# Block 1 of the output weights in tiles of another kind, in a one-core decoder layer

## The chip, the cores and the metric

One Trainium2 chip, one core. The time of a kernel is the device time of one launch in microseconds (us); the table gives the median of three runs. The profile is of one more execution, with its own time.

## The reference

One layer of a decoder on 1024 rows (and 16 learned rows ahead of them) of width 1024, all in float32:

```
u   = rmsnorm(h);  q, k, v, xr, yr = split(u @ w_in)
att = sliding-window attention with sinks (8 heads, 2 kv heads, window 128)
xr  = causal conv of width 4;  r, i = sigmoid(block-diagonal gates of xr)
hr  = scan h[t] = a[t] h[t-1] + sqrt(1 - a^2) * (i * xr),  a = exp(-8 r softplus(-lam))
h  += rmsnorm(concat(att, gelu(yr) * hr) @ w_out)
h  += rmsnorm(relu(rmsnorm(h) @ w_ff1)^2 @ w_ff2)
```

w_out is 1024 x 1024: eight blocks of 128 rows (kc = 0 to 7), of which 0 to 3 meet attention outputs and 4 to 7 meet the gated recurrence.

## The kernel before

Every float32 product is made of three products of a shorter format (`mm3`, lines 122 to 128): an operand is split into a high half, a cast on ScalarE (ACT, line 95) or VectorE (DVE, line 97), and a low half, the rest, always on DVE (line 98). Line 124 multiplies high by high, 125 and 126 the two mixed terms. So each block of w_out is loaded into a raw tile (`load_wo`, line 744, issued on SP's queue), its high half is cast, its low half is subtracted (`split_wo`), and then PE (TensorE) may use it in the output projection (`out_mm`, lines 787 to 797).

SBUF is cut into tiles of seven kinds, each with a fixed count (line 55): raw 2, ws 4, a 16, b 17, c 8, d 4, e 2. A tile is taken when a new name is given one of its kind, and it is free after the last reader of its old name. The 16 tiles a hold the normalized, transposed input u (high and low, 8 pairs) until the last projection of u is done. Of the two tiles e, one holds the raw gate weights (`graw`, line 683), until they are split, and the other their high half (`gh`, line 691), which PE reads in all four `gates(c)`.

The order on each engine isn't the order of the code: a scheduler orders the instructions of each engine when the program is built, from the priorities (the order of the code), the dependences and the release of tiles. Each engine then runs its own list strictly in order and waits for semaphores; a wait of one instruction holds all behind it on that engine. The projection of t = 0 to 3 uses two banks each of the four kinds of PSUM tiles (pt, o, acc, s) at once, since their first four blocks are given ahead (`out_mm(t, pos[t], range(4))`).

The time around the change: gates (PE, with sigmoids on ACT that empty the banks, line 82), the last projection y3 of u on PE with its copies on DVE (line 640), decay and recurrence (`decay`, `recur`: exponentials, square roots and table loads on ACT, products and scans on DVE, lines 728 to 730), gelu and gate products (line 736), then the output projection with a norm per 128 rows (`out_norm`, lines 803 to 825: squares at 810, scaling by the post-mix gain `gmix_b` at 816, adding x at 819, storing at 820, the second norm at 822 and 824) and transposes (`u2_tiles`: PE at 836, evictions on ACT at 847 and on DVE at 841). While it runs, the first FFN weights are loaded and split ahead (`early`, line 925).

Of the kernel before, what the change touches and what calls it, by code (L numbers as in the profile page):

```python
# [10 lines left out]
F32R = mybir.dt.float32r  # L11
# [5 lines left out]
P = 128  # L17
D = 1024
# [19 lines left out]
def hybrid_layer(  # L38
# [19 lines left out]
    def slot(tag, shape, dt=F32):  # L58
        uid[0] += 1
        return slab.tile(shape, dt, tag=tag, name=f"{tag}{uid[0]}", bufs=bufs[tag])  # L60

    def pair(tag, shape):
        return slot(tag, shape, F32R), slot(tag, shape, F32R)
# [29 lines left out]
    def split(hi, lo, src, eng=None):  # L93
        if eng is None:
            nc.scalar.copy(hi, src)  # L95
        else:
            eng.tensor_copy(hi, src)
        low = nc.vector.tensor_tensor(lo, src, f32(hi), op=ALU.subtract).ins  # L98
        mark[0] = low.name
        return low  # L100
# [648 lines left out]
    def split_wo(kc, tag, eng=None):  # L749
        wo[kc] = pair(tag, [P, D])  # L750
        split(wo[kc][0], wo[kc][1], wo_raw[kc], eng)
# [11 lines left out]
    load_wo(2, "d")  # L763
    load_wo(3, "raw")
    split_wo(0, "ws", nc.vector)
    for kc in range(1, 4):
        split_wo(kc, "a")
    for cp in (2, 3):
        at[0][cp] = pair("b", [P, 2, 512])
# [8 lines left out]
        rec_out(c, 1)  # L778


    gmix_b = slot("e", [P, D])
    nc.scalar.dma_start(gmix_b, g_post_mix[0].partition_broadcast(P))
    t4_dram = dpool.tile([P, 2, 4, 512], F32, name="t4_dram")

# [2 lines left out]
    def out_mm(t, po, kcs):  # L787
        half, o = t // 4, (t % 4) * P
        s = slice(o, o + P)
        for n in range(2):  # L790
            c = slice(512 * n, 512 * n + 512)
            for kc in kcs:
                ah, al = at[half][kc // 2]
                mm3(
                    po[n], (ah[:, kc % 2, s], al[:, kc % 2, s]),
                    (wo[kc][0][:, c], wo[kc][1][:, c]), kc == 0, kc == KC - 1,
                )

    def out_banks(t):
        tag = ("pt", "o", "acc", "s", "pt", "acc", "s", "pt")[t]  # L800
        return [bank(tag), bank(tag)]

    def out_norm(t, po):
        xr = slot("d", [P, D])
        nc.sync.dma_start(xr, x[t * P : (t + 1) * P, :])
        h = slot("raw", [P, D])
        ssq = [small.tile([P, 1], F32, name=f"sq{n}", tag=f"sq{n}") for n in range(2)]
        for n in range(2):
            c = slice(512 * n, 512 * n + 512)
            nc.scalar.activation(  # L810
                h[:, c], po[n], AF.Square, scale=RMS_SC, accum_out=ssq[n]
            )
        rs = rstd_of(ssq)
        for n in range(2):
            c = slice(512 * n, 512 * n + 512)
            nc.vector.scalar_tensor_tensor(
                h[:, c], po[n], rs, gmix_b[:, c], op0=ALU.mult, op1=ALU.mult
            )
        nc.vector.tensor_tensor(h, h, xr, op=ALU.add)
        nc.sync.dma_start(out[t * P : (t + 1) * P, :], h)  # L820
        ssq2 = small.tile([P, 1], F32, name="ssq", tag="ssq")
        nc.scalar.activation(xr, h, AF.Square, scale=RMS_SC, accum_out=ssq2)
        rs2 = rstd_of([ssq2])
        nc.vector.tensor_scalar(xr, h, rs2, None, op0=ALU.mult)
        return xr

    def u2_tiles(t, xn):
        half = t // 4
        if u2f[half][0] is None:
            u2f[half] = [slot("c", [P, 2, 512]) for _ in range(4)]  # L830
        o = (t % 4) * P
        for k4 in range(0, KC, 4):
            pt = bank("o", (P, 4, P))
            for i in range(4):
                kc = k4 + i
                nc.tensor.transpose(pt[:, i, :], xn[:, kc * P : (kc + 1) * P], ident)  # L836
            for i in range(0, 4, 2):
                kc = k4 + i
                dst = u2f[half][kc // 2]
                if k4:  # L840
                    nc.vector.tensor_tensor(
                        dst[:, :, o : o + P], pt[:, i : i + 2, :],
                        g_ffn_col[:, kc : kc + 2].to_broadcast([P, 2, P]), op=ALU.mult,
                    )
                    continue
                for n in range(2):
                    nc.scalar.activation(
                        dst[:, n, o : o + P], pt[:, i + n, :], AF.Copy,
                        scale=g_ffn_col[:, kc + n : kc + n + 1],
                    )  # L850
# [13 lines left out]
    def operand(tiles):  # L864
        pairs = []
        for t_ in tiles:
            hi, lo = pair("b", [P, 2, 512])
            split(hi, lo, t_)
            pairs.append((hi, lo))
        return pairs  # L870
# [54 lines left out]
    def early(b, p0, hl):  # L925
        raw = slot("raw", [P, 2, 4, P])
        for k in range(2):
            w1_load(raw[:, k], b, p0 + k, 0, 1)
        split(*hl, raw)
        return {p0 + k: (hl[0][:, k], hl[1][:, k]) for k in range(2)}  # L930
# [47 lines left out]
    ESH = [P, 2, 4, P]  # L978
# [11 lines left out]
    for t in range(8):  # L990
        po = pos[t] if t < 4 else out_banks(t)
        out_mm(t, po, range(4 if t < 4 else 0, KC))
        for t_ in {4: (0,), 5: (2,), 6: (4,), 7: (5,)}.get(t, ()):
            u2_tiles(t_, xns[t_])
        xns[t] = out_norm(t, po)
        for t_ in {4: (1,), 5: (3,), 7: (6,)}.get(t, ()):
            u2_tiles(t_, xns[t_])
        if t == 4:
            a11_early.update(early(0, 0, pair("a", ESH)))
        if t == 5:  # L1000
            b11 = operand(u2f[0][0:2])
            a12_early.update(early(1, 0, pair("ws", ESH)))
        if t == 6:
            b21 = operand(u2f[0][2:4])
            hl = slot("b", ESH, F32R), slot("e", ESH, F32R)
            a11_early.update(early(0, 2, hl))

    for p in range(2):
# [353 lines left out]
```

## Time and profile before

| what | value |
|---|---|
| time, median of 3 runs | 961.89 us (961.67 to 962.27) |
| time of the profiled execution | 959.9 us |
| span, first to last instruction | 957.9 us |
| granted TensorE clock, mean | 0.999 |
| busy: PE / DVE / ACT / POOL | 940.8 / 669.9 / 501.1 / 157.0 us |

The span is a little shorter than the time of the execution that it belongs to; what lies around it is launch and end. In the rows by time, a row has its start, its length, engine, line, operation, written and read tiles (buffer numbers left out), sizes, and in brackets the idle time of the engine before it with what ended it. A PE row is longer than the step from one matmul to the next, since matmuls overlap. The steps of such rows, not their lengths, tell PE's rate.

### The profile page before, as it was taken

The numbers are of one execution on the slowest core, as the hardware profiler recorded it, in microseconds if no ns is written. First come the engines' busy times: TensorE is split into PE (matmuls) and PEld (weight loads), VectorE is DVE, ScalarE is ACT, GpSimd is POOL, SyncE is SP. The second block draws the span as 40 slices with busy tenths as digits, with TensorE's granted clock in tenths as the row PEclk, the third lists the DMA queues.
The fourth block names the chain that finished last, engine by engine and source line by source line (L and its number), as shares of the span: only waits on it lengthen the run. The fifth ranks groups of instructions, "written<-read, shape, count | busy, mean of one in ns | idle before, by whom it ended". The sixth has DMA issues, their size and how long they took to land.

```text
span 957.9 us, 12381 instructions
## 1 busy us (share of the span) xinstructions
PE 940.8 (98%) x4654; PEld 789.2 (82%) x4654; DVE 669.9 (70%) x945; ACT 501.1 (52%) x822; POOL 157.0 (16%) x202
## 2 busy tenths in 40 slices
PE   7999999999999999999999999999999999999997
PEld 6999998888788877888888888888888888888886
DVE  5579989755955796575655556568557676779884
ACT  7556676469634563443555565654433343435441
POOL 4015656600021100000111001100111100003020
PEclk9999999999999999999999999999999999999999
DMA  8111101112235457675646466744677866567422
GB/s 289 51 49 41 38 9 45 38 62 67 87 133 176 141 181 236 190 260 188 212 154 219 155 195 188 234 156 122 161 181 191 199 219 195 178 193 159 112 87 88
DMA packets 85626, 140.74 MB, mean 147 GB/s; under 512 B 5784, under 2 KB 48936, under 8 KB 85568
## 3 DMA queue, kind: packets, MB, share of 16 engines
q1 hardware_dynamic: 75104, 108.51, 35.7%
q0 software_dynamic: 9600, 29.36, 11.9%
q10 hardware_dynamic: 864, 2.10, 0.6%
q8 instruction: 36, 0.59, 0.3%
q14 instruction: 22, 0.18, 0.1%
HBM read 115.70 MB, written 23.07 MB: 145 GB/s over the span
## 4 chain that ended last, share of the span: by engine, by line
PE 93%; ACT 3%; DVE 1%; issue 1%; DMA 0%; POOL 0%; DVEq 0%; SPq 0%; ACTq 0%
PE ps_acc L124 11%; PE ps_acc L125 11%; PE ps_acc L126 11%; PE ps_s L126 6%; PE ps_pt L124 6%; PE ps_s L125 6%; PE ps_s L124 6%; PE ps_pt L126 6%; PE ps_pt L125 6%; PE ps_o L124 5%; PE ps_o L126 5%; PE ps_o L125 5%; PE ps_o L585 1%; ACT c L82 1%; PE ps_o L836 1%
## 5 line engine op out<-in xcount | busy, mean ns | idle before, releaser
L95 ACT CAST ws<-raw 128x1024 fp32r<-128x1024 f32 (+1 forms) x70 | 71.8, 1026 | 120.5 <-PE ps_o L125 45.9
L98 DVE TENSOR_TENSOR ws<-raw,ws 128x1024 fp32r<-128x1024 f32 (+1 forms) x71 | 86.3, 1215 | 41.4 <-ACT ws L95 41.4
L124 PE MATMUL ps_acc<-a,ws 128*128 128x256 f32 (+2 forms) x256 | 85.2, 333 | 0.0
L125 PE MATMUL ps_acc<-a,ws 128*128 128x256 f32 (+2 forms) x256 | 84.9, 332 | 0.0
L126 PE MATMUL ps_acc<-a,ws 128*128 128x256 f32 (+2 forms) x256 | 84.8, 332 | 0.0
L98 DVE TENSOR_TENSOR b<-b,b 128x1024 fp32r<-128x1024 f32 (+2 forms) x48 | 57.6, 1201 | 29.3 <-PE ps_o L125 19.8
L95 ACT CAST ws<-e 128x1024 fp32r<-128x1024 f32 x42 | 43.9, 1045 | 58.2 <-PE ps_o L125 30.6
L95 ACT CAST b<-b 128x1024 fp32r<-128x1024 f32 (+2 forms) x48 | 49.4, 1030 | 35.0 <-DVE b L862 34.1
L98 DVE TENSOR_TENSOR ws<-e,ws 128x1024 fp32r<-128x1024 f32 x42 | 51.4, 1223 | 20.0 <-ACT ws L95 20.0
L575 POOL TENSOR_SCALAR_AFFINE_SELECT c<-c 128x512 fp32r<-128x512 f32 x64 | 55.7, 894 | 27.3 <-ACT c L95 15.3
L169 POOL TENSOR_TENSOR rs<-ms,half_pow 128x1 f32<-128x1 f32 (+1 forms) x29 | 21.3, 740 | 210.5 <-DVE ms L165 209.1
L126 PEld LDWEIGHTS ps_acc<-a,ws 128*128 128x128 f32 x256 | 48.2, 188 | 4.9
L124 PEld LDWEIGHTS ps_acc<-a,ws 128*128 128x128 f32 x256 | 48.2, 188 | 4.2
L125 PEld LDWEIGHTS ps_acc<-a,ws 128*128 128x128 f32 x256 | 48.2, 188 | 4.2
L124 PE MATMUL ps_acc<-ws,b 128*128 128x512 f32 (+1 forms) x120 | 46.3, 386 | 0.0
L125 PE MATMUL ps_acc<-ws,b 128*128 128x512 f32 (+1 forms) x120 | 46.1, 384 | 0.0
L126 PE MATMUL ps_acc<-ws,b 128*128 128x512 f32 (+1 forms) x120 | 46.0, 384 | 0.0
L125 PE MATMUL ps_pt<-ws,b 128*128 128x512 f32 x112 | 44.2, 395 | 0.6 <-DVE ws L98 0.6
L126 PE MATMUL ps_pt<-ws,b 128*128 128x512 f32 x112 | 43.9, 392 | 0.0
L124 PE MATMUL ps_pt<-ws,b 128*128 128x512 f32 x112 | 43.9, 394 | 0.0
L124 PE MATMUL ps_s<-ws,b 128*128 128x512 f32 x110 | 43.3, 395 | 0.0
L126 PE MATMUL ps_s<-ws,b 128*128 128x512 f32 x110 | 43.2, 393 | 0.0
(393 smaller groups left out, 2713.1 us busy)
## 6 DMA issues: line engine op xcount, KB each, us to landing
raw<-in_w_ff_dram SPq DMA_DIRECT2D x58, 512.0 KB, 4.3
e<-in_w_ff_dram SPq DMA_DIRECT2D x42, 512.0 KB, 4.1
raw<-in_w_in_dram SPq DMA_DIRECT2D x12, 512.0 KB, 3.9
d<-in_w_ff_dram SPq DMA_DIRECT2D x12, 512.0 KB, 3.8
s_dram<-d POOLq DMA_DIRECT2D x12, 512.0 KB, 3.9
e<-in_w_ff_dram POOLq DMA_DIRECT2D x10, 512.0 KB, 5.6
raw<-in_w_ff_dram POOLq DMA_DIRECT2D x10, 512.0 KB, 5.8
c<-in_x_dram SPq DMA_DIRECT2D x8, 512.0 KB, 8.1
```

The costliest lines, as they stand in the source:

```text
L82: ins = nc.scalar.activation(*args, **kwargs).ins
L95: nc.scalar.copy(hi, src)
L98: low = nc.vector.tensor_tensor(lo, src, f32(hi), op=ALU.subtract).ins
L124: nc.tensor.matmul(dst, lh, rh, start=start, stop=False, skip_group_check=True)
L125: nc.tensor.matmul(dst, lh, rl, start=False, stop=False, skip_group_check=True)
L126: last_mm[0] = nc.tensor.matmul(dst, ll, rh, start=False, stop=stop, skip_group_check=True).ins.name
L169: last_pow[0] = nc.gpsimd.tensor_tensor(rs[:n], ms[:n], half_pow[:n], op=ALU.pow).ins.name
L575: nc.gpsimd.affine_select(out=m[:, :, side, :], in_=f32(m)[:, :, 1, :], pattern=[[0, 4], [-sign, P]], compare_op=op, fill=0.0, base=0, cha ...
L585: nc.tensor.matmul(po[:, :, oc : oc + n], v, m[:, :, pc : pc + n], start=first and k == 0, stop=last and k == 1, skip_group_check=True,)
L836: nc.tensor.transpose(pt[:, i, :], xn[:, kc * P : (kc + 1) * P], ident)
```

## The change

Block 1 of w_out is split into the two tiles e instead of two tiles a: its high half takes the tile of the raw gate weights, its low half that of the high gate weights. Two later tiles go the other way: `gmix_b`, the post-mix gain spread over all partitions, and the low half of one early FFN block (`hl`) now take tiles a.

```diff
     split_wo(0, "ws", nc.vector)
-    for kc in range(1, 4):
+    split_wo(1, "e")
+    for kc in range(2, 4):
         split_wo(kc, "a")
...
-    gmix_b = slot("e", [P, D])
+    gmix_b = slot("a", [P, D])
     nc.scalar.dma_start(gmix_b, g_post_mix[0].partition_broadcast(P))
...
-            hl = slot("b", ESH, F32R), slot("e", ESH, F32R)
+            hl = slot("b", ESH, F32R), slot("a", ESH, F32R)
             a11_early.update(early(0, 2, hl))
```

Lines from 767 on carry a number higher by one after the change. No instruction is added or removed; the scheduler orders them otherwise. The first place is on ACT, from the gates to the end of the recurrence. raw_2758 is block 1, d_2760 block 2, raw_2762 block 3, d_2800 block 4:

```order
 L82 ACTIVATE c_2547<-ps_o_2558,prm 128x344
+L95 COPY e_2768<-raw_2758 128x1024
 L82 ACTIVATE c_2568<-ps_s_2569,prm 128x348
...
-L95 COPY a_2768<-raw_2758 128x1024
+L95 COPY a_2772<-d_2760 128x1024
 L82 ACTIVATE c_2605<-c_2605,m4sp 128x1040
 L82 ACTIVATE b_2745<-c_2642,m8sp 128x1040
-L95 COPY a_2772<-d_2760 128x1024
+L95 COPY a_2776<-raw_2762 128x1024
...
-L95 COPY a_2776<-raw_2762 128x1024
+L95 COPY a_2802<-d_2800 128x1024
```

Block 1's cast moves ahead among the sigmoids of the gates, and each of the blocks 2, 3 and 4 moves into the place of the one before it. On DVE the low halves move in the same way (2769 before the last gate product of line 715, then 2773, 2777 and 2803 each one place up). The cast of block 4 is followed by those of 5 to 7, behind which now stands the DMA of gmix_b (line 783 after the change), which stood before the gates.

The second place is PE at the start of the output projection, before the change (ps_pt_2849 and ps_pt_2850 are the two banks of the first 128 rows, ws_2764 and ws_2765 block 0, a_2768 and a_2769 block 1, b_946 and b_947 the first attention outputs):

```order
L125 MATMUL ps_pt_2849<-ws_2765,b_946 128x512
L126 MATMUL ps_pt_2849<-ws_2764,b_947 128x512
L124 MATMUL ps_pt_2849<-a_2768,b_946 128x512
L125 MATMUL ps_pt_2850<-ws_2765,b_946 128x512
L126 MATMUL ps_pt_2850<-ws_2764,b_947 128x512
L124 MATMUL ps_pt_2850<-a_2768,b_946 128x512
L125 MATMUL ps_o_2851<-ws_2765,b_946 128x512
```

and after it:

```order
L125 MATMUL ps_pt_2849<-ws_2765,b_946 128x512
L126 MATMUL ps_pt_2849<-ws_2764,b_947 128x512
L124 MATMUL ps_pt_2849<-e_2768,b_946 128x512
L125 MATMUL ps_pt_2849<-e_2769,b_946 128x512
L126 MATMUL ps_pt_2849<-e_2768,b_947 128x512
L124 MATMUL ps_pt_2849<-a_2772,b_1683 128x512
L125 MATMUL ps_pt_2850<-ws_2765,b_946 128x512
```

A bank now goes through blocks 0 and 1 and into block 2 before PE takes the next bank; before, PE went through six banks with block 0 and returned for block 1.

The third place is ACT during the norms, after the change (raw_3247 and raw_3366 are early FFN weights, ps_o_3191, 3229 and 3302 the first halves of the first three transposes):

```order
L848 ACTIVATE c_3188<-ps_o_3191,gcol 128x128 x2
L95 COPY a_3245<-raw_3247 128x1024
L823 ACTIVATE d_3207,ssq<-raw_3209 128x1024
L848 ACTIVATE c_3187<-ps_o_3229,gcol 128x128 x2
L848 ACTIVATE c_3188<-ps_o_3229,gcol 128x128 x2
L811 ACTIVATE raw_3320,sq_3321<-ps_acc_3252 128x512
L811 ACTIVATE raw_3320,sq_3322<-ps_acc_3253 128x512
L95 COPY ws_3364<-raw_3366 128x1024
L848 ACTIVATE c_3187<-ps_o_3302,gcol 128x128 x2
```

Before the change, the cast into a_3245 stood behind the eviction of ps_o_3229 and behind the square into d_3207, and the cast into ws_3364 behind the eviction of ps_o_3302. On SP the store of the fourth 128 rows (raw_3117) now stands ahead of the load of the fifth rows of x (d_3207), where it stood behind it.

## The prediction

> **What bounds the kernel now.** I read the head of the page first, then the waits of PE, then windows of single stages, and last the time-ordered rows of ACT, DVE and PE around the output projection. The page's first lines:
>
> ```profile
> span 957.9 us, 12381 instructions
> PE 940.8 (98%) x4654; PEld 789.2 (82%) x4654; DVE 669.9 (70%) x945; ACT 501.1 (52%) x822; POOL 157.0 (16%) x202
> ```
>
> PE is busy for all but 17.1 us. The change adds and removes no matmul, so it can win only gaps of PE, or add new ones. The view of the waits names the gaps (us in total, times, longest):
>
> ```profile
> PE ps_s L286 <- DVE d L213: 5.8, 1, 5.8
> PE ps_s L525 <- DVE negm L545: 1.7, 2, 1.3
> ...
> PE ps_acc L124 <- ACT a L1059: 0.7, 1, 0.7
> PE ps_pt L124 <- ACT a L95: 0.6, 1, 0.6
> PE ps_pt L125 <- DVE ws L98: 0.6, 1, 0.6
> ```
>
> The first two lie before the output projection, out of the change's reach. The last two are it: PE waits once for the high half of an output-weight block (ACT, L95) and once for a low half (DVE, L98). Windows of the stages (PE, PEld, DVE, ACT, POOL busy, then clock and DMA):
>
> ```profile
> 230.00:245.00 15.00, 13.96 (x60) 10.70 (x58) 15.00 (x14) 14.94 (x19) 0.00 (x0) 1.00 0.35 107
> 245.00:350.00 105.00, 104.89 (x487) 86.09 (x488) 76.94 (x110) 55.20 (x118) 12.91 (x25) 1.00 0.46 152
> 360.00:940.00 580.00, 580.00 (x2540) 472.42 (x2539) 387.74 (x404) 275.16 (x321) 52.83 (x61) 1.00 0.61 181
> ```
>
> Between 230 and 245 us ACT (14.94 of 15) and DVE (15.00 of 15) are both full and PE is not; that is the stage where one cast more or less decides. Afterwards PE is full again to the end, so microseconds gained by 245 should arrive at the end one for one, if no new gap opens.
>
> **The change, part by part.** The two gaps on PE:
>
> ```profile
> 231.98 0.63 PE L124 MATMUL ps_s<-ws,b 128*128 128x512 f32 x2
> 233.16 0.50 PE L125 MATMUL ps_pt<-ws,b 128*128 128x512 f32 x1 [0.56 <-DVE ws L98]
> 245.11 0.73 PE L124 MATMUL ps_pt<-a,b 128*128 128x512 f32 x2 [0.58 <-ACT a L95]
> ```
>
> *The high halves on ACT.* In the new order block 1 is cast between two sigmoids of the gates, and blocks 2, 3 and 4 take the places that blocks 1, 2 and 3 had.
>
> ```profile
> 203.96 0.58 ACT L82 ACTIVATE c<-ps_o,prm 128x344 f32<-128x344 f32 x1
> 206.12 0.55 ACT L82 ACTIVATE c<-ps_s,prm 128x348 f32<-128x348 f32 x1 [1.58 <-PE ps_s L126]
> 230.55 1.03 ACT L95 CAST a<-raw 128x1024 fp32r<-128x1024 f32 x1
> 233.60 1.04 ACT L95 CAST a<-d 128x1024 fp32r<-128x1024 f32 x1
> 244.03 1.03 ACT L95 CAST a<-raw 128x1024 fp32r<-128x1024 f32 x1
> ```
>
> The three last rows are blocks 1, 2 and 3. ACT idles from 204.54 to 206.12, 1.58 us, and the moved cast takes 1.03: hidden, if its data are there. Its load is the second of two rows merged here, with the time to landing of the eight loads of output weights under it:
>
> ```profile
> 189.78 10.43 SPq L744 DMA_DIRECT2D raw<-in_w_out_dram  x2
> DMA to landing us min/median/max: 3.2/3.2/4.1
> ```
>
> The second issue ends at 200.21, so it lands by about 204.3, just in time. Should it be 1 or 2 us late, the sigmoids behind it wait, and PE asks for their banks again only at the next set:
>
> ```profile
> 210.35 0.32 PE L124 MATMUL ps_s<-b,e 128*128 128x348 f32 x1
> ```
>
> That is 3.7 us after the bank's eviction ends at 206.67, so I cost this move at nothing; without that cover it is at most the cast's 1.03. Block 3's cast now stands at 233.60 instead of 244.03. Its load waits for block 1's raw tile, which is free after the early low half (below, 219.4); landing by 223.6, it is early by 10 us. PE's gap at 244.53 therefore goes: **0.58 us gained**. What stands at 244.03 now is block 4. Its load waits for block 2's tile, whose low half moves from 238.13 to 233.02 on DVE (next rows), so it is issued near 234.3 and lands by 238.4, ahead of 244.03.
>
> *The low halves on DVE.*
>
> ```profile
> 218.91 1.24 DVE L715 TENSOR_TENSOR c<-c,b 128x1040 f32<-128x1040 f32 x1 [3.69 <-ACT c L82]
> 221.79 0.69 DVE L640 COPY d<-ps_acc 128x512 f32<-128x512 f32 x1 [1.63 <-PE ps_acc L126]
> 231.89 1.22 DVE L98 TENSOR_TENSOR ws<-raw,ws 128x1024 fp32r<-128x1024 f32 x1
> 233.02 1.22 DVE L98 TENSOR_TENSOR a<-raw,a 128x1024 fp32r<-128x1024 f32 x1
> 238.13 1.22 DVE L98 TENSOR_TENSOR a<-d,a 128x1024 fp32r<-128x1024 f32 x1
> ```
>
> Block 1's low half needs the other tile of kind e, which holds the gate weights until the last gate product, about 218.1. It runs from there to 219.4 and pushes the L715 behind it by about 0.5 us, to 220.6; DVE then idles until 221.79 anyway. Cost: nothing. Block 0's low half (231.89, tile ws) keeps its place behind the same recurrence steps, so PE's other gap, 0.56 us, **stays**.
>
> *PE.* From the L125 at 233.16 on, both orders have 89 matmuls before the first one of block 4; the new order only uses blocks 0 to 3 bank by bank. The rows of before and the next block's first use:
>
> ```profile
> 254.74 0.39 PE L124 MATMUL ps_pt<-a,b 128*128 128x512 f32 x1
> 260.27 0.62 PE L124 MATMUL ps_pt<-a,b 128*128 128x512 f32 x2
> 258.26 1.14 ACT L95 CAST b<-d 128x512 fp32r<-128x512 f32 x2 [2.06 <-DVE d L736]
> ```
>
> With the gap gone PE is there at 254.16 and 259.69. Blocks 4 to 7 are split one place (1.1 us on DVE) earlier, so they are ready. The tightest input is one that does not move: the gated recurrence output cast at 258.26, ready at 258.88, with 0.81 us left for PE at 259.69 (1.39 before). No new gap, and if there were one it would be what is missing of that 0.81.
>
> *The post-mix gain.* Its broadcast load, issued at 194.68 before, now stands on ACT's queue behind the last cast of the weights:
>
> ```profile
> 255.15 1.05 ACT L95 CAST a<-raw 128x1024 fp32r<-128x1024 f32 x1
> DMA to landing us min/median/max: 3.7/3.7/3.7
> 269.60 1.41 DVE L816 SCALAR_TENSOR_TENSOR raw<-ps_pt,rs,e 128x512 f32<-128x512 f32 x2 [0.67 <-POOL rs L169]
> ```
>
> Issued by 256.2 and landing 3.7 later, near 260, it is 7 us or more ahead of its first reader, even if that moves up to 267.9. ACT pays 0.38 us for the issue in a time when it waits for L736. Cost: nothing.
>
> *The other a and e tiles.* The low half of an early FFN block takes an a tile in place of an e tile; the e tiles come free with the last output projection instead of with its norm. Both are earlier than their readers: no term.
>
> The sum: 0.58 + 0 + 0 = 0.6 us off the profiled execution, 959.9 to 959.3 (span 957.9 to 957.3). The median of the runs shown is 961.89, 2.0 above it; I take the difference over to the median: **961.3**.
>
> **Rivals.** *The evictions of the transposes become late (slower).* In the new ACT order the cast of the first early FFN weights stands ahead of the eviction of the second transposes, and the second such cast ahead of that of the third. Both wait for a DMA; PE waits for the eviction before the second half of the third transposes.
>
> ```profile
> 294.86 1.14 ACT L847 ACTIVATE c<-ps_o,gcol 128x128 f32<-128x128 f32 x4 [3.87 <-PE ps_o L836]
> 295.88 1.08 ACT L822 ACTIVATE d<-raw 128x1024 f32<-128x1024 f32 x1
> 298.52 1.05 ACT L95 CAST a<-raw 128x1024 fp32r<-128x1024 f32 x1 [1.48 <-DMA raw<-in_w_ff_dram]
> 300.89 1.04 PE L836 MATMUL ps_o<-ident,d 128*128 128x128 f32 x8
> ```
>
> Behind the cast now come the 1.08 and then the 1.14, so from the landing to the free bank it is 3.3 us. PE arrives at 300.89 - 0.58 + 0.5 for the first four transposes + 0.2 for the matmul now between = 301.0. Data that land later than 297.7 cost PE time, and later than 298.3 cost more than the 0.58 gained. At the 298.52 of before it loses 0.8 here; the like at the fourth transposes, 6 us on, I put at half of it. Together 1.2 lost, 0.6 gained: 962.5. Against it: the load waits for a store whose tile is written by the chain of norms that begins here:
>
> ```profile
> 267.47 0.60 ACT L810 ACTIVATE raw<-ps_pt 128x512 f32<-128x512 f32 x1 [5.65 <-PE ps_pt L126]
> 289.11 0.34 SPq L805 DMA_DIRECT2D d<-in_x_dram  x1
> 289.54 1.12 SPq L820 DMA_DIRECT2D out_dram<-raw  x1
> 294.84 0.94 SPq L859 DMA_DIRECT2D raw<-in_w_ff_dram  x2
> ```
>
> The first bank's last matmul moves up by five matmuls (1.16) beside the 0.58, so this chain starts 1.7 us earlier, and landing is at 296.8: 0.9 us to spare. The spare is an estimate, so the rival keeps 15%. The store also stands ahead of the load of x on SP now. The Trainium skill, "DMA: Bandwidth & Descriptors", section on queues, rings and completion order, says that each DMA engine consumes the descriptors of a queue in ring order; by that the store no longer stands behind the 512 KB of x and lands sooner still, which speaks against this rival. The 5.3 us from 289.54 to 294.84 fits it, but no row of before shows the other order.
>
> *The gain is eaten.* ACT's wait at L1059 (0.7) or an operand whose slack under a full PE I can't see takes back what PE gained: 961.9. For it: a full PE shows no slack, and 0.81 us was the least that I found. Against: what feeds PE from 245 to 350 is mostly released by PE and moves with it. 22%.
>
> *Both gaps go.* If block 0's low half came 0.5 us earlier as well, 0.56 more: 960.7. Against: DVE's rows ahead of it do not change. 8%.
>
> *Nothing is different,* because block 3's cast waits for its load after all: 961.9, counted with the second.
>
> **How the numbers follow.** Forecast 961.3: 55% (960.9 to 961.7 with the run-to-run spread of 0.3); gain eaten 22%, 961.9; late evictions 15%, 962.5, up to 964 if both loads land a microsecond or two later; both gaps 8%, 960.7. The range 960.4 to 963.0 leaves out the ends of the last two and whatever I have not seen. 0.2% is 1.9 us, about what a measurement of this kernel can tell from no change: faster than 959.97 needs more than all gaps in reach, 3%; slower than 963.81 needs the late evictions at their worst or a wait not seen, 8%; within, 89%.
>
> **What would show it.** In the new profile: the wait of PE for ACT, a, L95 gone from the list, that for DVE, ws, L98 still 0.5 to 0.6; a cast into e between two sigmoids near 204.5; block 3's high half near 233.6; PE's first transposes near 287.5 instead of 288.04; and no wait of PE for ACT c at L836 or L837. A wait there, or one for the cast at 258.26, makes me wrong on the slow side.

## The result and the profile after

The changed kernel takes 960.15 us (median of 22 runs, 957.97 to 962.51), the kernel before, run beside it, 961.53 us (22 runs, 959.94 to 963.69). The ratio is 0.9984, 95% interval 0.9976 to 0.9991: 1.5 us less, between 0.9 and 2.3. It was measured twice more (below): 0.9979 (0.9970 to 0.9989) and 0.9975 (0.9966 to 0.9984). So the change gains 1.5 to 2.4 us; the prediction said 0.6.

The head of the page of the changed kernel:

```profile
span 959.4 us, 12384 instructions
PE 942.2 (98%) x4654; PEld 792.1 (83%) x4654; DVE 670.1 (70%) x945; ACT 501.4 (52%) x822; POOL 157.6 (16%) x202
```

This one execution is longer than the profiled one of before (959.4 against 957.9), though its kernel is faster. Windows of 8 us around PE's two waits for negm (the softmax's negated row maximum, which DVE makes at L545), before and after (last three columns: granted clock, DMA share, GB/s):

```profile
155.00:163.00 8.00, 6.28 (x49) 5.84 (x48) 7.67 (x27) 6.16 (x21) 2.56 (x2) 1.00 0.24 68
```

```profile
155.00:163.00 8.00, 6.28 (x38) 5.92 (x37) 7.84 (x23) 4.91 (x17) 2.09 (x3) 0.79 0.23 68
```

The clock is 1.00 in the one and 0.79 in the other: 11 matmuls fewer in the same window. TensorE ran at half clock for 3.41 us there, which cost 1.5 us: from its first L525 to its first matmul with block 0 it took 170.80 us in the one and 172.32 in the other. It is no effect of the change: 6 of the 14 profiles of this study have the stretch, one of them of the unchanged kernel before. Single executions must therefore be compared by stages. From here on S is the stage from the first matmul with block 0 to the first transposes.

The waits of PE after (us in total, times, longest):

```profile
PE ps_s L286 <- DVE d L213: 5.8, 1, 5.8
PE ps_s L525 <- DVE negm L545: 1.7, 2, 1.3
PE ps_o L286 <- DVE d L213: 1.2, 1, 1.2
PE ps_acc L124 <- ACT a L1060: 0.7, 1, 0.7
PE ps_pt L125 <- DVE ws L98: 0.6, 1, 0.6
```

The wait for ACT a L95 is gone, that for DVE ws L98 is there as before, and none for the evictions at L837 has come. The two casts that moved on ACT, block 1's into e and block 3's (this execution runs 2.77 us behind the one of before here, 233.58 against 230.81):

```profile
207.17 1.08 ACT L95 CAST e<-raw 128x1024 fp32r<-128x1024 f32 x1
236.37 1.04 ACT L95 CAST a<-raw 128x1024 fp32r<-128x1024 f32 x1
```

Both stand where they were forecast, 204.4 and 233.6 in the time of before. The windows that were shown of before:

```profile
230.00:245.00 15.00, 14.44 (x63) 11.44 (x62) 15.00 (x13) 14.91 (x16) 0.00 (x0) 1.00 0.33 107
245.00:350.00 105.00, 105.00 (x490) 86.17 (x489) 77.55 (x110) 56.95 (x121) 13.54 (x25) 1.00 0.44 146
360.00:940.00 580.00, 579.67 (x2541) 473.04 (x2540) 387.97 (x405) 275.31 (x322) 53.07 (x62) 1.00 0.61 182
```

PE is busy 14.44 of 15 us where it was 13.96, and full behind that as before. By this view the gain is about half a microsecond, and the prediction right. But a row of PE is longer than its step, and busy time hides what a step takes. PE's rows by time, before (the rows of the gaps themselves stand in the prediction):

```profile
230.81 0.39 PE L124 MATMUL ps_pt<-ws,b 128*128 128x512 f32 x1
...
244.13 0.40 PE L125 MATMUL ps_acc<-a,b 128*128 128x512 f32 x1
...
245.67 0.39 PE L124 MATMUL ps_o<-a,b 128*128 128x512 f32 x1
...
288.04 0.27 PE L836 MATMUL ps_o<-ident,d 128*128 128x128 f32 x1
```

and after:

```profile
233.58 0.39 PE L124 MATMUL ps_pt<-ws,b 128*128 128x512 f32 x1
...
235.94 0.50 PE L125 MATMUL ps_pt<-ws,b 128*128 128x512 f32 x1 [0.56 <-DVE ws L98]
...
289.87 0.27 PE L837 MATMUL ps_o<-ident,d 128*128 128x128 f32 x1
```

S has 240 steps in both. It takes 288.04 - 230.81 = 57.23 us before and 289.87 - 233.58 = 56.29 after: **0.94 us less, not 0.58**. Before, the three steps from 244.13 to 245.67 take 1.54 us; at 0.2317 us each they would take 0.695. The gap thus cost 0.85 us. Its idle time is counted from the modelled end of the last row, 0.40 us long, and the step that restarts is slow as well. The rest of the steps in S average 0.2314 us before and 0.2311 after, which makes the other 0.09.

### The profile page after: what moved, and what is told of

Read it like the earlier page. It is cut to its first block, busy times and chain, and to the rows that moved or that the text cites. A ratio compares the mean times of both kernels' runs of the same rounds, so it can differ in the third digit from the quotient of the medians.

```text
span 959.4 us, 12384 instructions
## 1 busy us (share of the span) xinstructions
PE 942.2 (98%) x4654; PEld 792.1 (83%) x4654; DVE 670.1 (70%) x945; ACT 501.4 (52%) x822; POOL 157.6 (16%) x202
## 4 chain that ended last, share of the span: by engine, by line
PE 90%; DMA 3%; DVE 3%; issue 2%; ACT 2%; POOL 0%; DVEq 0%; SPq 0%; ACTq 0%; POOLq 0%
PE ps_acc L124 10%; PE ps_acc L125 10%; PE ps_acc L126 10%; PE ps_pt L125 7%; PE ps_pt L126 7%; PE ps_pt L124 6%; PE ps_s L126 6%; PE ps_s L125 6%; PE ps_s L124 6%; PE ps_o L125 5%; PE ps_o L126 5%; PE ps_o L124 5%; DMA d<-in_w_ff_dram 2%; PE ps_o L585 1%; DMA s_dram<-d 1%
## 5 line engine op out<-in xcount | busy, mean ns | idle before, releaser
L95 ACT CAST ws<-raw 128x1024 fp32r<-128x1024 f32 (+1 forms) x70 | 71.8, 1025 | 122.4 <-PE ps_o L125 42.1
L98 DVE TENSOR_TENSOR ws<-raw,ws 128x1024 fp32r<-128x1024 f32 (+1 forms) x71 | 86.1, 1213 | 41.1 <-ACT ws L95 41.1
L124 PE MATMUL ps_acc<-a,ws 128*128 128x256 f32 (+2 forms) x256 | 85.9, 336 | 0.0
L98 DVE TENSOR_TENSOR b<-b,b 128x1024 fp32r<-128x1024 f32 (+2 forms) x48 | 57.6, 1200 | 27.0 <-PE ps_o L125 17.5
L95 ACT CAST ws<-e 128x1024 fp32r<-128x1024 f32 x42 | 43.9, 1045 | 58.9 <-PE ps_o L125 30.2
L95 ACT CAST b<-b 128x1024 fp32r<-128x1024 f32 (+2 forms) x48 | 49.4, 1030 | 35.9 <-DVE b L863 34.9
L98 DVE TENSOR_TENSOR ws<-e,ws 128x1024 fp32r<-128x1024 f32 x42 | 51.4, 1223 | 20.6 <-ACT ws L95 20.6
L126 PEld LDWEIGHTS ps_acc<-a,ws 128*128 128x128 f32 x256 | 48.8, 191 | 4.9
L124 PEld LDWEIGHTS ps_acc<-a,ws 128*128 128x128 f32 x256 | 49.0, 191 | 4.1
L125 PEld LDWEIGHTS ps_acc<-a,ws 128*128 128x128 f32 x256 | 48.9, 191 | 4.2
L124 PE MATMUL ps_acc<-ws,b 128*128 128x512 f32 (+1 forms) x120 | 46.3, 385 | 0.0
L124 PE MATMUL ps_pt<-ws,b 128*128 128x512 f32 x112 | 43.8, 393 | 0.0
L124 PE MATMUL ps_s<-ws,b 128*128 128x512 f32 x110 | 43.3, 396 | 0.0
```

The lines of the kernel that those rows point to most:

```text
L124: nc.tensor.matmul(dst, lh, rh, start=start, stop=False, skip_group_check=True)
L125: nc.tensor.matmul(dst, lh, rl, start=False, stop=False, skip_group_check=True)
L126: last_mm[0] = nc.tensor.matmul(dst, ll, rh, start=False, stop=stop, skip_group_check=True).ins.name
```

## The experiments

**The change again, the cast alone, the wait alone, and the other gap.** The first four ran on one chip with the same 28 runs of the kernel before. T is the theory of the prediction with its new price: one wait of PE less, 0.85 to 0.94 us.

The changed kernel again (e1), no edit:

> The changed kernel once more. S is the stretch of TensorE from the first matmul with block 0 of the output weights (L124, ps_pt <- ws) to the first transposes of the next stage (L837): 57.23 us in the profiled run before, 56.29 in the one after. Theory T (the whole effect is that TensorE no longer waits for block 3's high half; the wait showed 0.58 us idle, but from start to start it cost 0.85 to 0.94): S is 56.3 again, and the time is 0.9 us below before's (ratio 0.9990, somewhat higher than the 0.9984 measured). Rival R1 (half of the gain comes from elsewhere, such as fewer half-clock stretches of TensorE): S is the same, but the ratio is 0.9984 or lower again, and the profile has fewer half-clock stretches than before's. The stretch of 3.4 us at half clock near 157 us, in after's profile alone so far, comes and goes by R1's opposite: if it is there in every run of the changed kernel, the change has a cost that neither theory names.

Measured: S 56.28; 958.49 us, ratio 0.9979 (0.9970 to 0.9989). There is no half-clock stretch near 157 us in this profile, so the change doesn't bring it each time. For R1, by which the changed kernel has fewer of them, there is no sign either: two of its three profiles have one, and one of the two of before. T's 0.9990 is missed from below.

The kernel before with only block 3's cast moved to GpSimd (e2):

```diff
-    for kc in range(1, 4):
-        split_wo(kc, "a")
+    split_wo(1, "a")
+    split_wo(2, "a")
+    split_wo(3, "a", nc.gpsimd)
```

> The kernel before, with all its tiles and its bank order; only block 3's high half is cast by GpSimd instead of ScalarE, so that it is not behind the six gelus. Theory T: TensorE's wait for ACT a L95 (0.58 idle) is gone with no tile moved, S falls from 57.23 to 56.3 to 56.4, and the time is 0.8 to 0.95 us below before's (ratio 0.9990). Rival R2 (the bank-by-bank order or the moved tiles make the gain): S stays at 57.1 to 57.3 and the ratio is 1.0000, even where the wait is gone. What could spoil it: GpSimd takes over 5 us for the cast, and TensorE waits for it instead (a wait with the releaser POOL a L97).

```profile
231.39 0.39 PE L124 MATMUL ps_pt<-ws,b 128*128 128x512 f32 x1
...
287.67 0.38 PE L837 MATMUL ps_o<-ident,d 128*128 128x128 f32 x2
```

S is 56.28 with no tile moved by hand and 14 of PE's matmuls in other places of its order: closing the wait makes the whole gain of S, and R2 falls. GpSimd's cast took 1.90 us. But the ratio is 0.9977 (0.9968 to 0.9986), 2.2 us, where T allows 0.95.

The changed kernel with block 3's cast back between the last two gelus (e3):

```diff
-    for kc in range(2, 4):
-        split_wo(kc, "a")
+    split_wo(2, "a")
...
+    wo[3] = pair("a", [P, D])
+    high3 = nc.scalar.copy(wo[3][0], wo_raw[3]).ins
+    nc.vector.tensor_tensor(wo[3][1], wo_raw[3], f32(wo[3][0]), op=ALU.subtract)
...
+    behind(gelu[2, 1], high3)
```

> The changed kernel with all its tiles as they are, but with block 3's cast on ScalarE put back to its old place between the last two gelus. Theory T: TensorE's wait for block 3's high half is back (0.4 to 0.7 us idle), S rises from 56.29 to 57.1 to 57.3, and the time is that of before (ratio 1.0000). Rival R2/R3 (the moved tiles or the bank order make the gain): S stays near 56.3 to 56.5 and the ratio is 0.9990, wait or not.

```profile
243.16 0.40 PE L125 MATMUL ps_acc<-e,b 128*128 128x512 f32 x1
244.01 0.49 PE L124 MATMUL ps_pt<-a,b 128*128 128x512 f32 x1 [0.45 <-ACT a L776]
...
287.56 0.27 PE L843 MATMUL ps_o<-ident,d 128*128 128x128 f32 x1
```

The wait is back, 0.45 us idle, and S with it: 57.04, a step of 0.85 in place of 0.23 and a slow restart. T is right about S but for 0.06 us. Yet the time isn't that of before: 958.81 us, ratio 0.9984 (0.9975 to 0.9994). A kernel that gains 0.19 us in S is 1.5 us faster.

The changed kernel with block 0's low half ahead of two steps of the recurrence on DVE (e4):

```diff
+    load_wo(0, "raw")
+    split_wo(0, "ws", nc.vector)
+    low0 = mark[0]
...
+        if c == 0:
+            behind(low0, s2)
+        if c == 1:
+            behind(low0, s1)
```

> The changed kernel, with block 0's low half taken by VectorE straight after its cast and ahead of two scan preparations (L728, L729), so that the other gap (0.56 us idle before L125 ps_pt <- ws, DVE ws L98) closes. By T, priced from start to start, that gap costs 0.8 us, not 0.56: S falls from 56.29 to 55.4 to 55.6, and the time by 0.8 (ratio to before 0.9981). If the idle time were the price, S would be 55.73. If VectorE's two moved steps then come late for the gates or the scans, a new wait of TensorE shows and S falls by less.

```profile
256.18 0.50 PE L126 MATMUL ps_pt<-a,b 128*128 128x512 f32 x1 [0.38 <-DVE b L98]
```

The gap at the start of S is gone, and the recurrence that was pushed back costs another: S is 56.10, the third case. The ratio is 0.9971 (0.9959 to 0.9982), the best of the study: 2.8 us below before, of which S explains 1.1.

**A control (e5), and the change a third time (e6).** All four kernels were 1.0 to 1.7 us faster than S says. Either the runs of before are measured too long, or something outside S is faster in every one of them.

> The kernel before, unchanged, run as if it were the changed one, since the changed kernel (ratio 0.9984, then 0.9979), the one with the cast alone (0.9977) and the one with the wait restored (0.9984) all came out 0.7 to 1.3 us lower than stretch S explains (0.95, 0.95 and 0.19 us). S must be 57.2. Theory C1 (something in every one of those kernels outside S is faster than in before): the ratio is 1.0000 within 0.0007. Theory C2 (a run is worth some 0.8 us less when it stands in the place of the changed kernel, whatever the kernel): the ratio is 0.9990 to 0.9993, and the changed kernel's own share is what S says, 0.95 us.

Measured: 961.45 us against 961.38, ratio 0.9999 (0.9989 to 1.0008). That is C1's ratio, but the interval still reaches C2's 0.9990 to 0.9993.

> The changed kernel a third time, beside the control on the same chip. S is 56.3. By C1 its ratio is 0.998 again, and 0.998 to the control too; by C2 its ratio is 0.998 and the control's 0.999, so that it stands 0.9990 to the control. The half-clock stretch of 3.4 us between the two waits for negm (there in 2 of the 6 profiles so far, the changed kernel's first and the one with the cast on GpSimd, worth 1.5 us each time) may come or not in any kernel.

Measured on the same chip: 958.70 us, 0.9975 (0.9966 to 0.9984), S 56.30. To the control's 961.45 us it stands at 0.9971, where C2 asked for 0.9990. C1 holds: some 1.5 us lie outside S (0.6 to 2.4 by the interval).

**Where it lies.** From the wait for ACT at L1059 near 354 us to the end, PE's rows are the same by kind of tile, one after the other, in all these kernels. I took the step from each matmul to the next and compared them one by one between profiles, where both are under 0.26 us: some 2615 steps. Longer ones are waits and are left out. They come and go in single runs: in sum they are 1.13 us more in the control than in before, 0.64, 1.69 and 0.58 more in the three profiles of the changed kernel, and between 0.08 less and 2.36 more (e4) in the others. One stretch shows it well, 578 steps without a wait, from an L124 that reads ws to another, late in the program. Before and after:

```profile
768.56 0.40 PE L124 MATMUL ps_s<-ws,b 128*128 128x512 f32 x1
...
901.78 0.39 PE L124 MATMUL ps_o<-ws,b 128*128 128x512 f32 x1
```

```profile
770.32 0.40 PE L124 MATMUL ps_s<-ws,b 128*128 128x512 f32 x1
...
903.36 0.39 PE L124 MATMUL ps_o<-ws,b 128*128 128x512 f32 x1
```

The first takes 133.22 us, the second 133.04. That is no scatter: the control took 133.22 too, the two repeats of the changed kernel 133.04 and 133.04. Single steps differ by 3.4 ns on average between before and after, some up, some down, but by 0.5 ns between two runs of before. In sum the changed kernel is ahead by 0.97, 0.95 and 0.99 us in its three profiles; the control is behind by 0.01. From the end of S to 354 us the two kernels differ by 0.01 to 0.07.

What differs there is where the tiles lie. In the programs as built, 59 of 243 b tiles, 74 of 89 e, 9 of 103 raw and 10 of 81 a lie in another buffer of their kind after the change, since a tile takes the buffer that came free first and the change alters that order. The kernel with the cast on GpSimd has 42 b tiles elsewhere, for the same reason. Of the 2614 steps, the 350 in whose neighbourhood every tile read lies where it lay add up to 0.00 us, the other 2264 to -0.97. That is no proof: singly those 350 change too, by nearly 3 ns on average, and with the neighbourhood drawn otherwise (from a step's own two matmuls to ten on either side) the sum of such steps comes out between -0.25 and 0.1 us.

One more run was made for the other gap (e7), beside the control: e4's edit, and on top of it

```diff
+        if c == 3:
+            behind(scan[1].name, s1)
...
+        if c == 1:
+            behind(mark[0], scan[3])
```

> The changed kernel with block 0's low half early as in the run before, and with the scans held in their old order, so that the low half of the second gate block is done before the last scan: in the last try it came late and TensorE waited 0.38 us for it (S 56.10 instead of 55.4). Theory T (start to start, each of the gaps is worth 0.8 us): no idle TensorE is left in S, S falls to 55.4 to 55.5, 1.8 below before's, and the time is 0.8 below the changed kernel's. If a gap is worth only its idle time, S would be 55.7. If VectorE simply has no room, another of its results comes late and S stays at 55.9 to 56.2.

```profile
254.25 0.40 PE L125 MATMUL ps_pt<-a,b 128*128 128x512 f32 x1
254.80 0.50 PE L126 MATMUL ps_pt<-a,b 128*128 128x512 f32 x1
...
259.40 0.50 PE L124 MATMUL ps_pt<-a,b 128*128 128x512 f32 x1 [0.41 <-ACT b L95]
```

S is 56.53, more than in any of the three cases: DVE has no room, and two small gaps came in place of one (the first, a step of 0.55, shows no idle time at all). 959.29 us, 0.9978 (0.9969 to 0.9987). By chance all its tiles lie where those of the changed kernel lie, and its 578 steps take 133.04.

**Moving tiles alone (e8 to e10).** Now only the places were changed, in the kernel before:

```diff
     nc.scalar.dma_start(gmix_b, g_post_mix[0].partition_broadcast(P))
+    spare = slot("b", [P, D])
+    nc.gpsimd.memset(spare[:, :1], 0.0)
```

> The kernel before, and ahead of the stage of the feed-forward weights one unused tile of the gate kind (tag b) is taken, one column of it set by GpSimd, and given back: TensorE, ScalarE and VectorE issue the same instructions in the same order with the same waits, but 65 tiles lie in another buffer of the same kind, and 1220 of the 2750 matmuls behind S read one of them. S and its two waits must be as before (57.2). Theory B (the place of a tile in SBUF sets the pace of the matmuls that read it, and the changed kernel's 0.97 us behind S come from 59 moved b tiles, 74 moved e tiles, 9 raw and 10 a): the matmuls with moved tiles keep another pace, by 2 to 4 ns each up or down, the same in every run, and the sum is off by 0.2 to 1 us to either side; those with tiles in their old places keep theirs to 0.1 ns on average. Theory P (the pace follows from when stage S ends, not from where tiles lie): the pace is that of before everywhere, 0.5 ns apart as two runs of before are, and the sum is under 0.05 us.

```profile
768.70 0.39 PE L124 MATMUL ps_s<-ws,b 128*128 128x512 f32 x1
...
901.63 0.39 PE L124 MATMUL ps_o<-ws,b 128*128 128x512 f32 x1
```

S 57.22 with both waits; 132.93 us for the 578 steps, 0.95 us less over all 2615, and 959.40 us, ratio 0.9986 (0.9975 to 0.9997). Tiles in other buffers, and nothing else but one column set by GpSimd, gain in the old kernel what the changed kernel gains behind S. Theory P falls, and B holds in the sum. It doesn't in the single step: the 958 steps with all tiles in their old places change by 2.0 ns each as well, though only by 0.13 us in sum.

> The same with three unused tiles held at once, which gives a third arrangement: 49 b tiles elsewhere, 884 matmuls read one. Theory B: again another sum, off by 0.1 to 1 us to either side from before's, and a time that moves with it. Theory P: the pace of before, sum under 0.05 us, ratio 1.0000.

With three tiles held: S 57.24, 0.22 us less behind S (133.30 for the 578 steps, so slower there and faster elsewhere). 961.59 us, 1.0006 (0.9993 to 1.0018). A third arrangement, a third pace, but no gain in time that could be told: 0.2 us is too little for that, and this program has 0.3 us more around its span.

> The changed kernel with the one unused tile: S stays at 56.3, and 1220 matmuls behind it read a tile in another buffer than in the changed kernel. Theory B: the pace behind S, which was 0.97 us in all below before's in three profiles of the changed kernel (0.96, 0.98, 0.96), comes out another, by 0.2 us or more to either side. Theory P: it stays 0.95 to 0.99 us below before's.

Measured: S 56.29; the steps behind it are 0.72 us below before's, 0.25 off the changed kernel's 0.97, as B asked for. 959.54 us, 0.9986 (0.9974 to 0.9998).

**A forecast by places (e11, e12).** The last two have e4's places for all that matmuls read, and another S. On top of e4's edit, one moves block 4's low half to GpSimd (shown), the other block 3's:

```diff
+        wo[4] = pair("a", [P, D])
+        nc.scalar.copy(wo[4][0], wo_raw[4])
+        nc.gpsimd.tensor_tensor(wo[4][1], wo_raw[4], f32(wo[4][0]), op=ALU.subtract)
```

> Block 0's low half early, as in the run that had S at 56.10 with one wait of 0.38 us left (for a gate block's low half that VectorE reached late), and now block 4's low half on GpSimd, which is idle there, so that VectorE is 1.1 us less behind. Theory T: that wait goes too and S has no step of TensorE over 0.25 us left; 240 steps of 0.231 give S = 55.45, 1.8 below before's. If GpSimd is slower than 6 us for the subtraction, TensorE waits for it at about 22.5 us into S. 80 raw tiles lie elsewhere than in the earlier run; by theory B only the b, a, e and ws tiles are read by matmuls, so the pace behind S is that of the earlier run: from the first L124 matmul near 768.7 to the one near 901.4, 578 steps, 132.68 us (before 133.22, changed kernel 133.04).

> The same with block 3's low half on GpSimd in place of block 4's. TensorE asks for it early, some 6 us into S, and may wait up to 2 us for GpSimd there, so S is between 55.5 and 57.5. Its tiles lie exactly where they lay in the earlier run with block 0's low half early, all of them. Theory B: whatever S is, the pace behind it is the earlier run's: 132.68 us for the 578 steps, 127.08 us for the 551 steps from the L126 matmul near 568.5 to the L124 near 695.6, both to 0.02 us. Theory P: with another S, another pace.

The 578 steps took 132.68 and 132.68 us, the 551 steps 127.09 and 127.08 (before 127.52, changed kernel 127.38): theory B's numbers, given ahead. The rows of the second:

```profile
771.50 0.39 PE L124 MATMUL ps_s<-ws,b 128*128 128x512 f32 x1
...
904.18 0.39 PE L124 MATMUL ps_o<-ws,b 128*128 128x512 f32 x1
```

In S I was wrong about both: 58.37, not 55.45, and 57.93, not 55.5 to 57.5. GpSimd and DVE, rows by time of the kernel with block 4 on GpSimd, and under them the same DVE step in e4:

```profile
246.91 2.46 POOL L785 TENSOR_TENSOR a<-d,a 128x1024 fp32r<-128x1024 f32 x1 [60.23 <-ACT a L784]
```

```profile
247.37 2.55 DVE L98 TENSOR_TENSOR b<-d,b 128x512 fp32r<-128x512 f32 x1 [0.27 <-ACT b L95]
```

```profile
248.07 0.68 DVE L98 TENSOR_TENSOR b<-d,b 128x512 fp32r<-128x512 f32 x1
```

DVE's subtraction of 512 columns, 0.68 us in e4, lasts 2.55, until 249.92, just behind GpSimd's end at 249.37. What was to free DVE for 1.1 us held it for 1.9, and PE waited 1.54 us for a low half and 0.80 for a cast. In the other, DVE's product at L729 took 2.79 us in place of 1.24, while GpSimd's subtraction took 3.94. The Trainium skill, "SBUF — State Buffer", section "Who interferes with whom", says that a VectorE instruction with two SBUF inputs contends with a GpSimd one that reads SBUF, and that the ports they share are an exclusive lock; these rows agree. Ratios 0.9995 (0.9984 to 1.0007) and 0.9994 (0.9984 to 1.0003).

**The account.** Against before, in us. Pace is the sum over the steps from 354 us on, with the difference of the 66 us ahead of them; the next column is the time of an execution less its span (2.04 on average before, 1.90 in the changed kernel, 1.70 to 2.33 in the others). Measured is the ratio on 961 us.

| kernel | S | pace | around | sum | measured |
|---|---|---|---|---|---|
| change (first) | -0.94 | -0.96 | -0.1 | -2.0 | -1.5 (-2.3 to -0.9) |
| e1, change | -0.95 | -0.88 | -0.2 | -2.0 | -2.0 (-2.9 to -1.1) |
| e6, change | -0.93 | -0.91 | -0.2 | -2.0 | -2.4 (-3.3 to -1.5) |
| e2, cast on GpSimd | -0.95 | -0.76 | 0.0 | -1.7 | -2.2 (-3.1 to -1.3) |
| e3, wait restored | -0.19 | -0.77 | -0.3 | -1.3 | -1.5 (-2.4 to -0.6) |
| e4, low half early | -1.13 | -1.33 | -0.3 | -2.8 | -2.8 (-3.9 to -1.7) |
| e5, control | 0.00 | 0.01 | 0.0 | 0.0 | -0.1 (-1.1 to 0.8) |
| e7, scans held | -0.70 | -0.90 | -0.1 | -1.7 | -2.1 (-3.0 to -1.2) |
| e8, before, tiles moved | -0.01 | -1.03 | 0.0 | -1.0 | -1.3 (-2.4 to -0.3) |
| e9, before, moved otherwise | 0.01 | -0.21 | 0.3 | 0.1 | 0.6 (-0.7 to 1.7) |
| e10, change, tiles moved | -0.94 | -0.78 | -0.3 | -2.0 | -1.3 (-2.5 to -0.2) |
| e11, low half of block 4 | 1.14 | -1.37 | -0.3 | -0.5 | -0.5 (-1.5 to 0.7) |
| e12, low half of block 3 | 0.70 | -1.28 | -0.3 | -0.9 | -0.6 (-1.5 to 0.3) |

Every sum lies in its interval; S alone lies outside it in nine of the thirteen. The intervals are some 2 us wide, and the sums leave out the single waits named above, which is right only if these come alike in all kernels; no run shows that they do.

One rule of the addresses shows when the programs are set against each other: places a multiple of 256 bytes apart act alike. From 354 us on, e3 and e10 read other buffers in 1212 of 2628 matmuls, each 16640 or 33280 bytes away, both multiples of 256, and their steps are 0.5 ns apart on average, as those of two runs of one program are. e2 differs from these two in 540 and 1062 matmuls, all but 20 by such multiples, and steps like them too (0.6 and 0.7 ns apart). The changed kernel differs from e3 by 24960 bytes, 128 over a multiple, in 628 matmuls, and is 3.1 to 3.2 ns apart. The ends of the 578 steps in e3 and in e10, 133.20 and 133.19 us (e2: 133.19):

```profile
767.66 0.40 PE L124 MATMUL ps_s<-ws,b 128*128 128x512 f32 x1
...
900.86 0.39 PE L124 MATMUL ps_o<-ws,b 128*128 128x512 f32 x1
```

```profile
767.66 0.40 PE L124 MATMUL ps_s<-ws,b 128*128 128x512 f32 x1
...
900.85 0.39 PE L124 MATMUL ps_o<-ws,b 128*128 128x512 f32 x1
```

No run was made to test this rule. Open are which remainders are fast and how they act; since steps with unmoved tiles change too, what the other engines read and write at the time may count. Open is also why the time around the span differs between programs. Faster than both kernels by its steps is e4: 0.2 us in S and 0.4 in the pace below the change, though its one profile has the most single waits, and by time alone, 958.10 against 958.49 us on the same chip, the two can't be told apart.

## Why the prediction was wrong

- **The order on ACT, DVE and PE** came out as worked: block 1's cast hidden between the sigmoids, block 3's cast ten microseconds earlier, the wait for ACT a L95 gone, that for DVE ws L98 unchanged, no new gap.
- **"0.58 us gained"** was the right gap at the wrong price. The idle time in brackets runs from a modelled end. From start to start the gap cost 0.85 us, and S became shorter by 0.94. e3 shows the price again: 0.45 idle, 0.75 in S.
- **"The other a and e tiles ... no term"** is the step that failed. It asked only whether tiles come free in time. The change hands the buffers out in another order, and the 2615 steps behind S are then 0.37 ns shorter each on average: 0.9 to 1.0 us, as much as the gap. e8 shows it with tiles alone, e11 and e12 by a forecast.
- **"Microseconds gained by 245 should arrive at the end one for one"** held for S, but a PE that is full has no fixed pace, and I took it for fixed. A third, small part, 0.1 us, lies around the span, which I left out.
- **The rivals**: no eviction of the transposes came late, and nothing was eaten. "Both gaps go" named almost the right size for a wrong reason: the second gap stayed.
- **The base and the range.** The forecast was 1.15 us above the 960.15 measured, and 0.36 of that is the base: three runs of before gave 961.89, 22 runs 961.53. The range took 0.3 us for the spread from run to run, after three runs within 0.6 us. 22 runs spread over 3.8 to 4.5 us; of this the profiles show up to 3.1 at the start (PE's first L525 comes between 59.1 and 62.2 us) and 1.5 by the half-clock stretch.

## What to carry to other kernels

Price a gap of TensorE by the starts around it less the usual steps, not by the idle time of a view. Where tiles take whichever buffer is free first, an edit of tile kinds or of order deals out other buffers to everything behind it; on this kernel, full of matmuls, the arrangements tried lay up to 1.4 us of 960 apart, so compare the steps of a stretch that the edit doesn't touch, and make a control that only moves tiles, before a gain of 0.1% is put down to the edit's purpose. And where single executions scatter by more than the effect, compare stages by their rows: S and the 578 steps repeat to 0.02 us.

## What the hardware showed that I had not expected

- **The pace of matmuls depends on where tiles lie**: the same 578 steps took between 132.68 and 133.30 us, by the arrangement, and the same to 0.01 us in every profile of one arrangement; places a multiple of 256 bytes apart gave the same steps. The Trainium skill, "TensorE: Matmul & The Clock Gate", section "Step-by-step: what each phase is for", says that loading the next weights takes no SBUF bandwidth from the running matmul; no run here tests that by itself, but the step of a stream of matmuls does depend on the places of tiles, by 2 to 4 ns of 231 up or down.
- **Half clock after short waits**: 3.41 us at half clock followed two waits of 0.46 to 0.49 and 1.26 us close together, in 6 of 14 profiles, at 1.5 us each; the same two waits stand in the other eight without it. What sorts them is a grid. Counted from the clock's first rise, its changes lie on whole steps of 3.413 us (42, 43 or 276 of them, for example). In the six profiles one such step holds 1.66 to 1.75 us of idle TensorE, and the next ran at half clock; until TensorE's work ends, no other step in any profile holds more than 1.60, and none was followed by half clock. The section "HAM oscillation — how this bites in real kernels" of the same page of the Trainium skill gives as the abstract rule that idle gaps of over about 3.4 us must be avoided; here less than 2 us of idle time within one step was enough.
- **A DVE step held by GpSimd**: 2.55 us in place of 0.68.
